# A two-layer decoder trunk on one core: 17 of the 22 gate/up tile pairs of the feed-forward input as seven products of half blocks

## The chip, the core and the metric

The kernel runs on one core of a Trainium2 chip. A core has a matrix engine (PE, with PEld for its weight loads), a vector engine (DVE), a scalar engine (ACT), a general engine (POOL, GpSimd) and a sync engine (SP); each takes its instructions in a fixed order and they wait for one another by semaphores. 16 DMA engines move data between HBM and the on-chip memories SBUF and PSUM. The metric is the device time of one execution in microseconds (us).

## The reference

Two layers, each a norm, a combined input projection, three token mixers (windowed attention, short convolution, a grouped state-space model), a gated merge, an output projection, and then the feed-forward part that the change is about. With 512 tokens, width 1024 and 2816 hidden features, that part is:

```python
h = rmsnorm(x, norm_ffn[i])
gt, up = jnp.split(h @ w_ffn_in[i], 2, axis=-1)
x = x + (jax.nn.silu(gt) * up) @ w_ffn_out[i]
```

All is float32.

## The kernel before

Features lie on the 128 partitions and tokens on the free axis, so x is 8 tiles of 128x512. Each large product is made of three matmuls in the matrix engine's rounded float32 format: every operand is split into a high part (rounded) and a low part (what the rounding left), and high·high, high·low and low·high are summed in PSUM (mm3, L151; gemm runs it over 8 blocks of the inner dimension).

Weights come in chunks of 128x1024 (8 blocks of 128x128; some of 512 columns). SP loads a chunk into a `raw` tile (2 buffers), ACT writes its high part `whi` (L132), DVE its low part `wlo` (L134, 3 buffers each); `chunk()` keeps AHEAD = 2 chunks prepared beyond the one in use.

The feed-forward part of a layer goes through 22 tiles f of 128 hidden features in four groups (FGROUPS: 8, 8, 2 and 4 tiles). For a tile, 24 matmuls of 512 columns give the gate's product `pfg` and 24 more the up product `pfu`, in PSUM banks of a pool of four ("mm"). DVE multiplies both by the token scale of the norm (`ga`, `ub`, L239), ACT takes a tanh (`th`, L959), DVE finishes the silu, multiplies, and ACT and DVE split the hidden tile into high and low parts (L171, L172). After each group its hidden tiles are multiplied by the rows of the output weights (`pfo`, 8 tiles of 128 features) and DVE adds the result to `xres`. The last products of layer 2 go by halves of the tokens, with matmuls of 256 columns.

The order of each engine's instructions is set when the program is built, by a scheduler that plays the program through; buffers of one tag are handed out in that order, and an instruction that takes a buffer over waits for the last reader of what was in it.

Of the kernel before, what the change touches and what calls it, by code (L numbers as in the profile page):

```python
# [16 lines left out]
P = 128  # L17
# [18 lines left out]
# how many units of other work lie between the steps of an octet, of a block of queries, and between these  # L36
# [18 lines left out]
def hybrid_kernel(ctx, tc, xin, wst, vec, ssp, ssb, sbt, cst, out):  # L55
# [6 lines left out]
    ap = ctx.enter_context(tc.tile_pool(name="ap", bufs=1))  # L62
# [4 lines left out]
    NU2 = 61  # L67
    NWP, NRAW, AHEAD = 3, 2, 2
# [22 lines left out]
    # the tables of the activation functions are there before the data  # L91
    A.activation(small([P, 1], "warm"), ones[:, 0:1], AF.Square)

    # the tensor engine's clock is up before the data
# [30 lines left out]
    def chunk_steps():  # L125
        if not raws:
            fetch_chunk()
        raw, cuts = raws.pop(0)
        hi = wp.tile([P, 1024], F32R, tag="whi", bufs=NWP, name="whi")
        lo = wp.tile([P, 1024], F32R, tag="wlo", bufs=NWP, name="wlo")  # L130
        for c in cuts:
            A.copy(hi[:, c], raw[:, c])  # L132
            yield
            V.tensor_tensor(out=lo[:, c], in0=raw[:, c], in1=hi[:, c].bitcast(F32), op=ALU.subtract)  # L134
# [12 lines left out]
    def mm3(o, w, x, start, stop):
        """o += w.T x for w, x given as (high, low) parts."""
        (wh, wl), (xh, xl) = w, x
        for i, (a, b) in enumerate(((wh, xh), (wh, xl), (wl, xh))):  # L150
            T.matmul(o, a, b, start=start and i == 0, stop=stop and i == 2)  # L151
# [34 lines left out]
    def norm_steps(ssum, got, n=NB, bank=auxps):  # L186
        """r[token, block] and r broadcast over partitions (in PSUM), from the partial sums of squares."""
# [74 lines left out]
    first = chunk_steps()  # L262
# [12 lines left out]
    # what is not needed yet does not go before the weights  # L275
# [3 lines left out]
    def u_products(ssum):  # L279
        """The input of the SSM, with the norm of the tokens worked out between its products."""  # L280
# [107 lines left out]
    def sincos_of(y):  # L388
# [168 lines left out]
    def ssm_octet(l, o, ut, store, yso):  # L557
        """Eight groups of the SSM, its steps apart for other work to run between them."""
# [20 lines left out]
        # C lambda^0..3 (imaginary part negated), lambda^1..4 B_bar turned  # L579
# [10 lines left out]
        # responses inside a chunk, D with them  # L590
# [26 lines left out]
        tcs = [tab[:, i, qt] for i in range(2)]  # L617
        # turned back by phi c, the recurrence is real: z_c = |lambda|^4 z_(c-1) + w_c
# [25 lines left out]
        # channels back on the partitions; tokens stay in the order (step, chunk)  # L644
# [61 lines left out]
    def attention(l, n, qkf, vs, kt, ot):  # L706
# [87 lines left out]
    for l in range(DEPTH):  # L794
# [24 lines left out]
        kt = [ap.tile([P, NKV, 2 * P], F32R, tag=f"kt{i}", bufs=1, name=f"kt{i}") for i in range(2)]  # L819
# [125 lines left out]
        xg, ssum = [], None  # L945
        for gi, (f0, f1) in enumerate(FGROUPS):
# [208 lines left out]
```

## Time and profile before

| | |
|---|---|
| time, median of 3 runs | 1594.62 us (1593.84 to 1596.13) |
| the profiled execution: span | 1592.0 us |
| PE busy | 1575.5 us, 99%, 7620 instructions |
| DVE busy | 994.8 us, 62% |
| ACT busy | 565.9 us, 36% |
| POOL busy | 119.0 us, 7% |
| DMA | 165.87 MB, mean 104 GB/s |
| DMA queues | hardware 157.35 MB (30.3% of the 16 engines' time), software, issued by POOL, 6.71 MB (2.0%) |

The span runs from the first to the last instruction on the chip; the rest of the time (2.6 us against the median) lies around it. "Busy" is the time in which at least one instruction of the engine ran; records of PE overlap, since matmuls are pipelined. In the parts below a row of the chain of waits gives start, duration, engine, tile, line and count; a row of the groups gives line, engine, operation, output <- inputs, shape, count, then total busy time and the mean in ns of one; "DMA issues" ends in the median us from issue to landing.

### The profile page before, as it was taken

How to read it: one execution, taken by the hardware profiler on the slowest of the kernel's cores; microseconds unless marked ns; L12 is line 12 of the kernel's file. 1: busy time of each engine (PE TensorE's matmuls, PEld its weight loads, DVE VectorE, ACT ScalarE, POOL GpSimd, SP SyncE). 2: the span in 40 equal slices, each digit the busy share in tenths (PEclk: the TensorE clock that was granted, in tenths of full speed). 3: DMA queues.
4: the chain of work that ended last, by engine and by line, in shares of the span. 5: the costliest groups of instructions: out<-in, count | busy, mean ns of one | idle time of the engine just before them, and what ended most of it. 6: DMA issues, size and time to landing. Idle time of an engine off the chain costs nothing.

```text
span 1592.0 us, 20211 instructions
## 1 busy us (share of the span) xinstructions
PE 1575.5 (99%) x7620; PEld 1301.7 (82%) x7620; DVE 994.8 (62%) x1986; ACT 565.9 (36%) x939; POOL 119.0 (7%) x231
## 2 busy tenths in 40 slices
PE   9999999999999999999999999999999999999996
PEld 7877788888888888888888778788888888888886
DVE  7976779746655345445658676887475643544546
ACT  4355433344432222222424554333443322222223
POOL 0301112210000000000030012212000000000001
PEclk9999999999999999999999999999999999999998
DMA  5422324323423322322433233333243323232231
GB/s 196 135 95 76 96 83 119 119 70 119 152 93 99 100 93 96 104 93 94 157 107 111 76 89 96 93 103 113 70 152 119 95 91 106 93 105 93 94 105 67
DMA packets 69985, 165.87 MB, mean 104 GB/s; under 512 B 18848, under 2 KB 24256, under 8 KB 69888
## 3 DMA queue, kind: packets, MB, share of 16 engines
q1 hardware_dynamic: 62944, 157.35, 30.3%
q0 software_dynamic: 6656, 6.71, 2.0%
q8 instruction: 60, 0.98, 0.2%
q10 hardware_dynamic: 288, 0.52, 0.1%
q14 instruction: 37, 0.30, 0.1%
HBM read 155.10 MB, written 5.24 MB: 101 GB/s over the span
## 4 chain that ended last, share of the span: by engine, by line
PE 98%; DVE 1%; DMA 0%; issue 0%; ACT 0%; SPq 0%; DVEq 0%
PE pg L151 17%; PE pfo L151 15%; PE pfu L151 15%; PE pfg L151 15%; PE pc L151 8%; PE py L151 8%; PE px L151 5%; PE pu L151 3%; PE pqb L151 3%; PE pkv L151 1%; PE pz L151 1%; PE pS L730 1%; PE po L776 1%; PE py L640 1%; PE pvv L614 1%; PE pT L764 1%
## 5 line engine op out<-in xcount | busy, mean ns | idle before, releaser
L132 ACT CAST whi<-raw 128x1024 fp32r<-128x1024 f32 (+1 forms) x298 | 287.8, 967 | 807.2 <-issue 194.2
L134 DVE TENSOR_TENSOR wlo<-raw,whi 128x1024 fp32r<-128x1024 f32 (+1 forms) x298 | 332.9, 1118 | 104.1 <-ACT whi L132 98.0
L151 PE MATMUL pg<-hi,whi 128*128 128x512 f32 x384 | 152.4, 397 | 0.0
L151 PE MATMUL pg<-lo,whi 128*128 128x512 f32 x384 | 150.3, 391 | 0.0
L151 PE MATMUL pg<-hi,wlo 128*128 128x512 f32 x384 | 150.1, 391 | 0.0
L151 PE MATMUL pfo<-lo,whi 128*128 128x512 f32 (+1 forms) x384 | 142.4, 371 | 0.0
L151 PE MATMUL pfo<-hi,wlo 128*128 128x512 f32 (+1 forms) x384 | 142.3, 371 | 0.0
L151 PE MATMUL pfo<-hi,whi 128*128 128x512 f32 (+1 forms) x384 | 140.9, 372 | 0.0
L151 PE MATMUL pfu<-hi,wlo 128*128 128x512 f32 x352 | 137.2, 390 | 0.0
L151 PE MATMUL pfu<-hi,whi 128*128 128x512 f32 x352 | 137.1, 390 | 0.0
L151 PE MATMUL pfu<-lo,whi 128*128 128x512 f32 x352 | 137.0, 389 | 0.0
L151 PE MATMUL pfg<-hi,whi 128*128 128x512 f32 x352 | 136.9, 389 | 0.0
L151 PE MATMUL pfg<-lo,whi 128*128 128x512 f32 x352 | 136.9, 389 | 0.0
L151 PE MATMUL pfg<-hi,wlo 128*128 128x512 f32 x352 | 136.9, 389 | 0.0
L239 DVE TENSOR_TENSOR xres<-xres,pfo 128x512 f32<-128x512 f32 (+1 forms) x72 | 44.0, 626 | 116.2 <-PE pfo L151 115.8
L239 DVE TENSOR_TENSOR ub<-pfu,rb 128x512 f32<-128x512 f32 x44 | 30.4, 691 | 108.6 <-PE pfu L151 108.6
L239 DVE TENSOR_TENSOR ga<-pfg,rb 128x512 f32<-128x512 f32 x44 | 30.4, 691 | 93.2 <-PE pfg L151 93.2
L151 PEld LDWEIGHTS pg<-hi,whi 128*128 128x128 f32 x384 | 72.1, 188 | 16.0 <-issue 1.0
L151 PEld LDWEIGHTS pg<-hi,wlo 128*128 128x128 f32 x384 | 72.1, 188 | 15.2
L151 PEld LDWEIGHTS pg<-lo,whi 128*128 128x128 f32 x384 | 72.2, 188 | 14.2
L151 PEld LDWEIGHTS pfo<-lo,whi 128*128 128x128 f32 x384 | 72.3, 188 | 12.5
L151 PEld LDWEIGHTS pfo<-hi,wlo 128*128 128x128 f32 x384 | 72.3, 188 | 12.5
(244 smaller groups left out, 3043.1 us busy)
## 6 DMA issues: line engine op xcount, KB each, us to landing
raw<-wst SPq DMA_DIRECT2D x240, 512.0 KB, 3.5
raw<-wst SPq DMA_DIRECT2D x56, 256.0 KB, 2.5
x<-xin SPq DMA_DIRECT2D x8, 256.0 KB, 5.1
bt<-sbt SPq DMA_DIRECT2D x8, 256.0 KB, 4.7
pt<-pfd SPq DMA_DIRECT2D x64, 32.0 KB, 4.1
mt<-kd POOLq DMA_DIRECT2D x64, 32.0 KB, 3.8
yd<-yj POOLq DMA_DIRECT2D x64, 32.0 KB, 2.8
xres<-xin SPq DMA_DIRECT2D x8, 256.0 KB, 3.8
```

Source lines behind the costliest of these rows:

```text
L132: A.copy(hi[:, c], raw[:, c])
L134: V.tensor_tensor(out=lo[:, c], in0=raw[:, c], in1=hi[:, c].bitcast(F32), op=ALU.subtract)
L151: T.matmul(o, a, b, start=start and i == 0, stop=stop and i == 2)
L239: V.tensor_tensor(out=out, in0=a, in1=b, op=op)
L614: T.matmul(pv[i][:, q], vt[i][:, q].rearrange("p g s -> p (g s)"), ut[:, q], start=True, stop=True)
L640: T.matmul(py[:, q, 1:NCK], flat(cl[i], q), xs[i][:, q, 0 : NCK - 1], start=False, stop=(i == 1),)
L730: T.matmul(pS[par][:, hp, keys], qt[a][rows, 2 * k + hp], kt[b][rows, k, keys], start=i == 0, stop=i == 2,)
L764: T.transpose(pT[:, h], st[h // 2][:, h % 2, kb * P : (kb + 1) * P], ident)
L776: T.matmul(po[64 * par : 64 * par + 64], v, pt[:, 2 * par : 2 * par + 2], start=kb == 0, stop=kb == len(pts) - 1,)
```

## The change

The groups become 6, 6, 6 and 4 tiles. The first five tiles of a layer (f < NPLAIN = 5) stay as they were, except that the activation is ACT's Silu in place of tanh and two steps of DVE. The other 17 go as a "pair" (`pair_tile`): gate and up weights are the two rows of a block matrix, the inner dimension is halved (4 blocks each), the tokens are halved (256 columns each), and the 2x2 block product is made of seven half-block products in place of eight, in Winograd's form of Strassen's scheme. So a pair is 7 x 4 x 3 = 84 matmuls of 256 columns, where a plain tile is 2 x 8 x 3 = 48 of 512.

For that each layer forms once, from the normed input (`halves_steps`), the halves of the tokens b11, b21, b22 and their sums t1 to t4, each split in high and low parts (DVE and ACT). Of the weights, the sums s1 to s4 are needed beside a11, a12 and a22: SP loads `r2` (a21, a11) from a new array wsp and POOL adds (a22, a21) to it by a DMA that accumulates (L149); DVE makes `r3` from it with two additions (L184, L185); SP loads `r1` (a11, a12) and `r4` (a22) as they are. ACT writes the high parts h1 to h4 (3 of 1024 columns, 1 of 512), DVE the low parts l1 to l4 (L162). While a pair's products run, the steps of a later pair's weights and the evaluation of the pair before are taken in turn (`beside`).

The seven products go to three PSUM tiles: `pb` (a11 b11, then s2 t2 and s3 t3 added on), `pc` (a22 t4) and `pd` (a12 b21 in one half, s1 t1 and s4 b22 in the other). ACT copies pb, the second half of pd, pb again and pc (128x256 each, L1092 to L1099) between the products; then DVE adds, ACT takes Silu (L1106), and DVE finishes (L240 is the last low part).

Buffers: raw 2 to 5, whi and wlo 3 to 5; the general pool `u2` 61 to 62, with a few tiles of other pools moved into it or into raw, whi and wlo. Three more loads of ACT's function tables appear in the program (4 in place of 1). The rest of the diff below the fence is naming, layout on the host and comments.

```diff
-FGROUPS = [(0, 8), (8, 16), (16, 18), (18, 22)]
+FGROUPS = [(0, 6), (6, 12), (12, 18), (18, 22)]
+NPLAIN = 5
+NF = FFN // P
+HS = S // 2
...
-    NU2 = 61
-    NWP, NRAW, AHEAD = 3, 2, 2
+    NU2 = 62
+    NHI, NLO, NRAW, AHEAD = 5, 5, 5, 2
...
     def fetch_chunk(queue=nc.sync, parts=1):
-        i = loaded[0]
+        i, n = items[loaded[0]]
         loaded[0] += 1
-        raw = wp.tile([P, 1024], F32, tag="raw", bufs=NRAW, name="raw")
-        n = sizes[i] // parts
+        if n is None:
+            r1, r2, r4 = wraw("r1"), wraw("r2"), u2([P, S], F32, "r4")
+            queue.dma_start(r2, wsp[i, :, 1024:2048])
+            queue.dma_start(r1, wsp[i, :, 0:1024])
+            nc.gpsimd.dma_start(r2, wsp[i, :, 2048:3072], accum_op=ALU.add)
+            queue.dma_start(r4, wsp[i, :, 2048 : 2048 + S])
+            raws.append((r1, r2, r4))
+            return None
...
+    def lo_of(lo, raw, hi):
+        V.tensor_tensor(out=lo, in0=raw, in1=hi.bitcast(F32), op=ALU.subtract)
+        return lo
+    def item_steps():
         if not raws:
             fetch_chunk()
-        raw, cuts = raws.pop(0)
-        hi = wp.tile([P, 1024], F32R, tag="whi", bufs=NWP, name="whi")
-        lo = wp.tile([P, 1024], F32R, tag="wlo", bufs=NWP, name="wlo")
-        for c in cuts:
-            A.copy(hi[:, c], raw[:, c])
-            yield
-            V.tensor_tensor(out=lo[:, c], in0=raw[:, c], in1=hi[:, c].bitcast(F32), op=ALU.subtract)
-            yield
-        ready.append((hi, lo))
+        got = raws.pop(0)
+        if len(got) == 2:
+            raw, cuts = got
+            hi, lo = whi(), wlo()
+            for c in cuts:
+                A.copy(hi[:, c], raw[:, c])
+                yield
+                lo_of(lo[:, c], raw[:, c], hi[:, c])
+                yield
+            ready.append((hi, lo))
+            return
+        r1, r2, r4 = got
+        a, b = slice(0, S), slice(S, 2 * S)
+        h1 = whi("h1")
+        A.copy(h1, r1)
+        r3 = wraw("r3")
+        V.tensor_tensor(out=r3[:, a], in0=r2[:, a], in1=r1[:, a], op=ALU.add)
+        V.tensor_tensor(out=r3[:, b], in0=r3[:, a], in1=r1[:, b], op=ALU.add)
+        yield
+        h2 = whi("h2")
+        A.copy(h2, r2)
+        p1 = (h1, lo_of(wlo("l1"), r1, h1))
+        yield
+        h3 = whi("h3")
+        A.copy(h3, r3)
+        p2 = (h2, lo_of(wlo("l2"), r2, h2))
+        yield
+        h4 = u2([P, S], F32R, "h4")
+        A.copy(h4, r4)
+        p3 = (h3, lo_of(wlo("l3"), r3, h3))
+        yield
+        p4 = (h4, lo_of(u2([P, S], F32R, "l4"), r4, h4))
+        part = lambda p, c: (p[0][:, c], p[1][:, c])
+        ready.append(
+            dict(a11=part(p1, a), a12=part(p1, b), s1=part(p2, a), s3=part(p2, b),
+                 s2=part(p3, a), s4=part(p3, b), a22=part(p4, a))
+        )
...
+        def halves_steps():
+            for j in range(KT // 2):
+                h1, h2 = u2([P, S], F32, "h1"), u2([P, S], F32, "h2")
+                for h, k in ((h1, j), (h2, j + KT // 2)):
+                    stt(h, xres[k], vcol(l, V_NF, k), rb2, ALU.mult, ALU.mult)
+                yield
+                b11, b12, b21, b22 = h1[:, :HS], h1[:, HS:], h2[:, :HS], h2[:, HS:]
+                t12, t34 = u2([P, 2, HS], F32, "t12"), u2([P, 2, HS], F32, "t34")
+                tt(t12[:, 0], b11, b12, ALU.subtract)
+                stt(t12[:, 1], t12[:, 0], -1.0, b22, ALU.mult, ALU.subtract)
+                tt(t34[:, 0], b22, b12, ALU.subtract)
+                stt(t34[:, 1], t12[:, 1], -1.0, b21, ALU.mult, ALU.subtract)
+                yield
+                first = u2([P, 2, HS], F32R, "b11")
+                A.copy(first[:, 0], b11)
+                tt(first[:, 1], b11, first[:, 0].bitcast(F32), ALU.subtract)
+                parts = []
+                for t in (h2.rearrange("p (a c) -> p a c", a=2), t12, t34):
+                    hi, lo = split(t, None, shape=(P, 2, HS))
+                    parts += [(hi[:, i], lo[:, i]) for i in range(2)]
+                    yield
+                b21_, b22_, t1, t2, t3, t4 = parts
+                ops.append(dict(b11=(first[:, 0], first[:, 1]), b21=b21_, b22=b22_, t1=t1, t2=t2, t3=t3, t4=t4))
+                yield
+        def hidden(ga, ub, hid):
+            tt(ga, ga, ub, ALU.mult)
+            hid.append(split(ga, None))
+        def plain_tile(f, hid):
+            pg, pu = mmps([P, S], "pfg"), mmps([P, S], "pfu")
+            for p_ in (pg, pu):
+                w = chunk()
+                gemm(p_, w, KC, xg2)
+                if f == 0:
+                    next(norm2)
+                yield
+            if f == 0:
+                nonlocal_rb.append(broadcast_of(rs_[1])[0])
+            r = nonlocal_rb[0]
+            ga, ub = u2([P, S], F32, "ga"), u2([P, S], F32, "ub")
+            tt(ga, pg, r, ALU.mult)
+            A.activation(ga, ga, AF.Silu)
+            tt(ub, pu, r, ALU.mult)
+            hidden(ga, ub, hid)
+            yield
+        def pair_tile(hid, beside):
+            if not ready:
+                load_chunk()
+            w = ready.pop(0)
+            pb, pc, pd = mmps([P, HS], "pb"), mmps([P, HS], "pc"), auxps([P, 2, HS], "pd")
+            ga, ub = u2([P, 2, HS], F32, "ga"), u2([P, 2, HS], F32, "ub")
+            def product(o, a, b, start=True):
+                n = len(ops)
+                for k in range(n):
+                    c = KC(k)
+                    mm3(o, (w[a][0][:, c], w[a][1][:, c]), ops[k][b], start and k == 0, k == n - 1, more=not start)
+                for g in list(beside):
+                    if next(g, "end") == "end":
+                        beside.remove(g)
+            product(pb, "a11", "b11")
+            A.copy(ga[:, 0], pb)
+            product(pd[:, 0], "a12", "b21")
+            product(pd[:, 1], "s1", "t1")
+            A.copy(ub[:, 1], pd[:, 1])
+            product(pb, "s2", "t2", start=False)
+            A.copy(ga[:, 1], pb)
+            product(pc, "a22", "t4")
+            A.copy(ub[:, 0], pc)
+            product(pd[:, 1], "s4", "b22", start=False)
+            product(pb, "s3", "t3", start=False)
+            def evacuated():
+                flat = lambda x: x.rearrange("p a c -> p (a c)")
+                tt(ga, ga, pd, ALU.add)
+                A.activation(ga, ga, AF.Silu)
+                yield
+                stt(ub, pb.unsqueeze(1).to_broadcast([P, 2, HS]), -1.0, ub, ALU.mult, ALU.subtract)
+                yield
+                hidden(flat(ga), flat(ub), hid)
+                yield
+            return evacuated()
+        nonlocal_rb = []
+        beside = []
         for gi, (f0, f1) in enumerate(FGROUPS):
             hid = []
             for f in range(f0, f1):
-                pg, pu = mmps([P, S], "pfg"), mmps([P, S], "pfu")
-                for p_ in (pg, pu):
-                    w = chunk()
-                    gemm(p_, w, KC, xg2)
-                    if f == 0:
-                        next(norm2)
-                if f == 0:
-                    rb2, _ = broadcast_of(rs_[1])
-                ga, ub, th = u2([P, S], F32, "ga"), u2([P, S], F32, "ub"), u2([P, S], F32, "th")
-                tt(ga, pg, rb2, ALU.mult)
-                A.activation(th, ga, AF.Tanh, scale=0.5)
-                tt(ub, pu, rb2, ALU.mult)
-                stt(ga, th, 1.0, ga, ALU.add, ALU.mult)
-                tt(ga, ga, ub, ALU.mult)
-                hid.append(split(ga, 0.5))
+                if f < NPLAIN:
+                    for _ in plain_tile(f, hid):
+                        if f == 0 and nonlocal_rb:
+                            rb2 = nonlocal_rb[0]
+                            prep = halves_steps()
+                        elif f > 0:
+                            for _ in range(3):
+                                next(prep, None)
+                    continue
+                if f == NPLAIN:
+                    for _ in prep:
+                        pass
+                if not ready:
+                    load_chunk()
+                if next_is_pair() and f + 1 < f1:
+                    beside.append(item_steps())
+                ev = pair_tile(hid, beside)
```

Where the instructions stand. **DVE, the plain tiles of layer 1.** Of before, from the first evaluation of a tile (`ga<-pfg` is tile 0's, `pfg_4473` and `pfg_4547` are those of tiles 1 and 2; `wlo` low parts of weights):

```order
L134 TENSOR_TENSOR wlo_4508<-raw_4505,whi_4507 128x1024
L239 TENSOR_TENSOR ga_4461<-pfg_4364,rb_4459 128x512
L239 TENSOR_TENSOR ub_4462<-pfu_4365,rb_4459 128x512
L243 SCALAR_TENSOR_TENSOR ga_4461<-th_4463,ga_4461 128x512
L239 TENSOR_TENSOR ga_4461<-ga_4461,ub_4462 128x512
L172 SCALAR_TENSOR_TENSOR lo_4470<-ga_4461,hi_4469 128x512
L239 TENSOR_TENSOR ga_4535<-pfg_4473,rb_4459 128x512
L134 TENSOR_TENSOR wlo_4552<-raw_4549,whi_4551 128x1024
L239 TENSOR_TENSOR ub_4536<-pfu_4474,rb_4459 128x512
```

Of after, the same place; `h1`, `h2`, `t12`, `t34` and `b11` are the halves and their sums, `r3` a weight sum of the first pair:

```order
L162 TENSOR_TENSOR wlo_4624<-raw_4621,whi_4623 128x1024
L313 TENSOR_TENSOR ga_4457<-pfg_4360,rb_4455 128x512
L313 TENSOR_TENSOR ub_4458<-pfu_4361,rb_4455 128x512
L184 TENSOR_TENSOR r3_4852<-r2_4844,r1_4843 128x512
L313 TENSOR_TENSOR ga_4457<-ga_4457,ub_4458 128x512
L185 TENSOR_TENSOR r3_4852<-r3_4852,r1_4843 128x512
L240 TENSOR_TENSOR lo_4464<-ga_4457,hi_4463 128x512
L317 SCALAR_TENSOR_TENSOR h1_4499<-xres_4063,vecs_72,rb_4455 128x512
L317 SCALAR_TENSOR_TENSOR h2_4500<-xres_4226,vecs_72,rb_4455 128x512
L162 TENSOR_TENSOR wlo_4691<-raw_4688,whi_4690 128x1024
L313 TENSOR_TENSOR t12_4503<-h1_4499 128x256
L313 TENSOR_TENSOR t34_4504<-h2_4500,h1_4499 128x256
```

Before, tile 0 is evaluated in five rows and then tile 1; after, the steps of the halves and the first pair's weights stand between. Further on, from the first pair's low part l1 to tile 2's `ga<-pfg` (`pfg_4581`), which frees a PSUM bank, it is 22 rows, and these are the last of them:

```order
L317 SCALAR_TENSOR_TENSOR h1_4651<-xres_4144,vecs_72,rb_4455 128x512
L317 SCALAR_TENSOR_TENSOR h2_4652<-xres_4308,vecs_72,rb_4455 128x512
L313 TENSOR_TENSOR t12_4655<-h1_4651 128x256
L313 TENSOR_TENSOR t34_4656<-h2_4652,h1_4651 128x256
L317 SCALAR_TENSOR_TENSOR t12_4655<-t12_4655,h2_4652 128x256
L313 TENSOR_TENSOR b11_4661<-h1_4651,b11_4661 128x256
L240 TENSOR_TENSOR lo_4665<-h2_4652,hi_4664 128x512
L317 SCALAR_TENSOR_TENSOR t34_4656<-t12_4655,h2_4652 128x256
L313 TENSOR_TENSOR ga_4668<-pfg_4581,rb_4455 128x512
```

**PE, around the first pair of layer 1.** Of before, from the end of tile 4's up product (`pfu_4696`) to the next tile:

```order
L151 MATMUL pfu_4696<-hi_4356,whi_4655 128x512
L151 MATMUL pfu_4696<-lo_4357,whi_4655 128x512
L151 MATMUL pfu_4696<-hi_4356,wlo_4656 128x512
L151 MATMUL pfg_4769<-hi_4070,whi_4699 128x512
L151 MATMUL pfg_4769<-lo_4071,whi_4699 128x512
L151 MATMUL pfg_4769<-hi_4070,wlo_4700 128x512
```

Of after, the end of the pair's `pd` (s1 t1) and what follows; `b11` holds both parts, so that "x2" is two matmuls, and `h4`, `l4` are the parts of a22:

```order
L225 MATMUL pd_4871<-hi_4765,l2_4861 128x256
L225 MATMUL pb_4869<-b11_4509,h1_4850 128x256 x2
L225 MATMUL pb_4869<-b11_4509,l1_4857 128x256
L225 MATMUL pb_4869<-b11_4574,h1_4850 128x256 x2
L225 MATMUL pb_4869<-b11_4574,l1_4857 128x256
L225 MATMUL pb_4869<-b11_4661,h1_4850 128x256 x2
L225 MATMUL pb_4869<-b11_4661,l1_4857 128x256
L225 MATMUL pb_4869<-b11_4728,h1_4850 128x256 x2
L225 MATMUL pb_4869<-b11_4728,l1_4857 128x256
L225 MATMUL pc_4870<-hi_4550,h4_4863 128x256
L225 MATMUL pc_4870<-lo_4551,h4_4863 128x256
L225 MATMUL pfo_4988<-hi_4463,whi_4972 128x512
```

Before, one plain tile follows the other; after, the products of the first pair follow tile 4, and the fourth product (`pc`) and the first output product `pfo_4988` are taken in turn (of its six hidden tiles those of the five plain ones come first, hi_4839 and lo_4840 of tile 4 as the fifth; the pair's own comes later).

**SP, the loads for that place.** Of before:

```order
L121 DMA raw_4653<-wst 128x1024
L121 DMA raw_4697<-wst 128x1024
L121 DMA raw_4727<-wst 128x1024
L121 DMA raw_4771<-wst 128x1024
L121 DMA raw_4801<-wst 128x1024
L121 DMA raw_4845<-wst 128x1024
```

Of after; `raw` of 768 columns are chunks of the output weights, `r1`, `r2` and `r4` belong to pairs (`r4_4845` to the first one, `r2_5179` to the second):

```order
L147 DMA r2_4844<-wsp 128x1024
L148 DMA r1_4843<-wsp 128x1024
L157 DMA raw_4970<-wst 128x768
L157 DMA raw_4976<-wst 128x768
L157 DMA raw_4982<-wst 128x768
L157 DMA raw_5008<-wst 128x768
L157 DMA raw_5034<-wst 128x768
L157 DMA raw_5060<-wst 128x768
L157 DMA raw_5086<-wst 128x768
L157 DMA raw_5112<-wst 128x768
L150 DMA r4_4845<-wsp 128x512
L147 DMA r2_5179<-wsp 128x1024
```

The first pair's `r2` and `r1` stand ahead of the eight chunks of the first group's output weights, its `r4` behind all eight.

More of the change, by code (lines that the diff above doesn't have):

```diff
@@ L54, in hybrid_kernel @@
 @with_exitstack
-def hybrid_kernel(ctx, tc, xin, wst, vec, ssp, ssb, sbt, cst, out):
+def hybrid_kernel(ctx, tc, xin, wst, wsp, vec, ssp, ssb, sbt, cst, out):
     nc = tc.nc
@@ L112, in hybrid_kernel, with wraw, whi, wlo @@
     raws = []
+    def wraw(name="raw", dt=F32):
+        return wp.tile([P, 1024], dt, tag="raw", bufs=NRAW, name=name)
+    def whi(name="whi", dt=F32R):
+        return wp.tile([P, 1024], dt, tag="whi", bufs=NHI, name=name)
+    def wlo(name="wlo", dt=F32R):
+        return wp.tile([P, 1024], dt, tag="wlo", bufs=NLO, name=name)
     def fetch_chunk(queue=nc.sync, parts=1):
-        i = loaded[0]
+        i, n = items[loaded[0]]
         loaded[0] += 1
-        raw = wp.tile([P, 1024], F32, tag="raw", bufs=NRAW, name="raw")
-        n = sizes[i] // parts
+        if n is None:
[6 more added lines that the diff above has]
+            return None
+        raw = wraw()
+        n //= parts
         cuts = [slice(j * n, (j + 1) * n) for j in range(parts)]
@@ L138, in load_chunk, with next_is_pair, mm3 @@
     def load_chunk():
-        for _ in chunk_steps():
+        for _ in item_steps():
             pass
+    def next_is_pair(n=0):
+        i = loaded[0] - len(raws) + n
+        return i < len(items) and items[i][1] is None
     def chunk():
-        while len(ready) <= AHEAD and (raws or loaded[0] < len(sizes)):
+        while len(ready) <= AHEAD and (raws or loaded[0] < len(items)) and not next_is_pair():
+            load_chunk()
+        if not ready:
             load_chunk()
         return ready.pop(0)
-    def mm3(o, w, x, start, stop):
+    def mm3(o, w, x, start, stop, more=False):
@@ L149, in mm3 @@
         (wh, wl), (xh, xl) = w, x
         for i, (a, b) in enumerate(((wh, xh), (wh, xl), (wl, xh))):
-            T.matmul(o, a, b, start=start and i == 0, stop=stop and i == 2)
+            T.matmul(o, a, b, start=start and i == 0, stop=stop and i == 2, skip_group_check=more)
     def gemm(o, w, kcols, xs):
@@ L261, in hybrid_kernel @@
     xg = []
-    first = chunk_steps()
+    first = item_steps()
     with tc.manual_schedule(engines={mybir.EngineType.DVE, mybir.EngineType.Activation}):
@@ L299, in u_evacuated @@
         for o in range(4):
+            if o % 2 == 0:
+                both = whi("uts", F32).rearrange("p (o q c) -> p o q c", o=2, q=4)
             u = u2([P, TJ, NCK], F32, "uperm")
@@ L522, in ssm_params @@
         qs = slice(l * NQ, (l + 1) * NQ)
-        b_c = cp.tile([P, 4, NQ, GRP], F32, tag="b_c", name="b_c")
+        b_c = wraw("b_c").rearrange("p (i q h) -> p i q h", i=4, q=NQ)
         with tc.issue_after(third.ins):
@@ L533, in ssm_tables @@
         qs = slice(l * NQ + half * nq, l * NQ + (half + 1) * nq)
-        tab = cp.tile([P, 2, nq, NCK], F32, tag="tab", name="tab")
-        store.append(tab)
-        tc_, tn_ = tab[:, 0], tab[:, 1]
+        tc_, tn_ = (wlo("tab", F32).rearrange("p (q c) -> p q c", q=nq) for _ in range(2))
+        store.append((tc_, tn_))
         V.memset(tc_[:, :, 0:1], 1.0)
@@ L616, in ssm_octet @@
         qt = slice((o % 2) * 4, (o % 2) * 4 + 4)
-        tcs = [tab[:, i, qt] for i in range(2)]
+        tcs = [tab[i][:, qt] for i in range(2)]
         s4 = lambda name: u2([P, 4, NCK], F32, name)
@@ L818, in hybrid_kernel @@
         vs = u2([P, NB, P], F32, "vs")
-        kt = [ap.tile([P, NKV, 2 * P], F32R, tag=f"kt{i}", bufs=1, name=f"kt{i}") for i in range(2)]
+        kt = [t[:, i] for t in [wraw("kt", F32R).rearrange("p (i v n) -> p i v n", i=2, v=NKV)] for i in range(2)]
         ot = [(u2([P, S], F32R, "oth"), u2([P, S], F32R, "otl")) for _ in range(4)]
@@ L1041, in _pkc, with _tiles, _pairs @@
     return w[:, c0:c1].reshape(k, P, c1 - c0).transpose(1, 0, 2).reshape(P, -1)
+def _tiles(i, l, f):
+    w = i["w_ffn_in"][l]
+    return [_pkc(w, c + f * P, c + (f + 1) * P) for c in (0, FFN)]
+def _pairs(i):
+    st = np.zeros((DEPTH * (NF - NPLAIN), P, 3072), np.float32)
+    for n in range(st.shape[0]):
+        g, u = _tiles(i, n // (NF - NPLAIN), NPLAIN + n % (NF - NPLAIN))
+        (a11, a12), (a21, a22) = ((w[:, :S], w[:, S:]) for w in (g, u))
+        st[n] = np.concatenate([a11, a12, a21, a11, a22, a21], 1)
+    return st
 def _weights(i):
@@ L1146 @@
         nc.dram_tensor(n, arrays[n].shape, F32, kind="ExternalInput").ap()
-        for n in ("xin", "wst", "vec", "ssp", "ssb", "sbt", "cst")
+        for n in ("xin", "wst", "wsp", "vec", "ssp", "ssb", "sbt", "cst")
     ]
```

54 lines of the change are left out of this document (38 added, 16 removed).

## Prediction

> **What bounds the kernel now.** I first read the shares of the chain of waits, then the chain in order of time where the feed-forward part begins, and at the places with matmuls of 256 columns:
>
> ```profile
> PE 98%; DVE 1%; DMA 0%; issue 0%; ACT 0%; SPq 0%; DVEq 0%
> ...
> 52.56 10.92 PE pkv L151 x91
> ...
> 442.13 5.44 PE pfg L151 x24
> 447.57 0.44 PE pr L215 x4
> 448.00 5.47 PE pfu L151 x24
> 453.47 5.44 PE pfg L151 x24
> 458.91 5.44 PE pfu L151 x24
> 464.35 5.44 PE pfg L151 x24
> 469.79 5.44 PE pfu L151 x24
> 475.23 5.44 PE pfg L151 x24
> ...
> 1552.57 15.53 PE pfo L151 x129
> ```
>
> The matrix engine is the chain, and in the feed-forward part one tile follows the other without a gap. 24 matmuls of 512 columns take 5.44 us: 226.7 ns each. Those of 256 columns take 10.92/91 = 15.53/129 = 120 ns. The other engines, by windows over the first two groups (columns: PE, PEld, DVE, ACT, POOL busy us, granted clock, DMA share, GB/s):
>
> ```profile
> 430.00:562.00 132.00, 132.00 (x590) 109.44 (x589) 63.68 (x87) 36.41 (x43) 0.00 (x0) 1.00 0.30 96
> 562.00:693.00 131.00, 131.00 (x580) 108.51 (x579) 60.55 (x73) 34.97 (x41) 0.00 (x0) 1.00 0.29 97
> ```
>
> DVE is busy under half of the stage, ACT a good quarter, DMA 0.30. So fewer PE cycles shorten the stage, as long as DVE, ACT and the loads keep up.
>
> **The matmuls.** A pair: before 48 x 226.7 = 10.88 us, after 84 x 120 = 10.08 us; 0.80 us less. 34 pairs: **-27.2 us**. The 7/8 of the scheme would give 1.36 us a pair, but 512 columns cost 106.7 ns more than 256, so each matmul has 13.3 ns that don't shrink, and there are 36 more. The rule that would make this smaller still, a gap per matmul, stands in the Trainium skill, "TensorE: Matmul & The Clock Gate", section "Wait — 56ns, not 53.3ns?": N/2.4 GHz plus about 2.5 ns. By it a pair would gain 48 x 215.8 - 84 x 109.2 = 1.19 us and the sum here be an estimated -40 us; the rows differ (226.7 and 120 ns), and I go by the rows. The output products keep 528 matmuls a layer whatever the groups: nothing.
>
> **DVE and ACT, steady state.** The durations, from the groups by shape:
>
> ```profile
> L134 DVE TENSOR_TENSOR wlo<-raw,whi 128x1024 fp32r<-128x1024 f32 x240 | 293.1, 1222 | 74.3 <-ACT whi L132 73.4 <-PE pq L709 0.6
> L239 DVE TENSOR_TENSOR ga<-ga,ub 128x512 f32<-128x512 f32 x44 | 30.5, 692 | 1.5
> L172 DVE SCALAR_TENSOR_TENSOR lo<-xres,vecs,hi 128x512 fp32r<-128x512 f32 x24 | 17.8, 747 | 4.8 <-ACT hi L171 4.8
> L239 DVE TENSOR_TENSOR apt<-b_c,pw 128x256 f32<-128x256 f32 x32 | 12.1, 419 | 0.0
> L132 ACT CAST whi<-raw 128x1024 fp32r<-128x1024 f32 x240 | 252.0, 1051 | 689.3 <-issue 185.0 <-PE pfo L151 160.4 <-PE pfg L151 137.5
> L132 ACT CAST whi<-raw 128x512 fp32r<-128x512 f32 x58 | 35.8, 620 | 117.9 <-PE pg L151 72.8 <-PE py L151 26.6 <-issue 9.2
> L171 ACT ACTIVATE hi<-ga 128x512 fp32r<-128x512 f32 x44 | 27.9, 634 | 31.0 <-DVE ga L239 31.0
> L180 ACT ACTIVATE sq<-xres 128x256 f32<-128x256 f32 x16 | 6.3, 414 | 10.5 <-DVE xres L239 10.5
> L92 ACT ACT_TABLE_LOAD x1 | 1.3, 1283 | 1.2 <-PEq L1144 1.2
> ```
>
> A pair costs DVE l1 to l3 3 x 1.22, l4 and two sums 3 x 0.69, evaluation 4 x 0.69: 8.5 us of 10.08. ACT: h1 to h3 3 x 1.05, h4 0.62, four copies 4 x 0.41, Silu and high part 1.27: 6.7 us. Both fit, but tighter than before (5.9 and 3.4 of 10.88), so I cost the pairs at PE's 10.08 us; every us by which DVE passes 10.08 would cost 34. Three more table loads (3 x 1.28 = 3.8 us of ACT) lie where ACT has idle time: nothing, at most 3.8. The buffers that were moved (rb, q, k and tables) touch the mixing part, where PE waits in no row of the chain; 0, with 3 us either way.
>
> **The plain tiles: a first wait.** In the order of after, `ga<-pfg` of tile 2, which frees the bank for tile 4, stands 22 rows behind l1. l1's buffer is free when PE ends tile 2's up product, 464.35 on the clock of before, plus ACT's h1 1.05: 465.40. The 22 rows are two of 1024 columns (2.44), four h1/h2 as L172's with a pointer (2.99), ten of 256 (4.19) and six of 512 (4.15): 13.8 us, to 479.2. How DVE goes through such rows shows the timeline:
>
> ```profile
> 455.56 0.68 DVE L239 TENSOR_TENSOR ub<-pfu,rb 128x512 f32<-128x512 f32 x1
> 456.16 0.68 DVE L243 SCALAR_TENSOR_TENSOR ga<-th,ga 128x512 f32<-128x512 f32 x1
> 456.87 0.69 DVE L239 TENSOR_TENSOR ga<-ga,ub 128x512 f32<-128x512 f32 x1
> ```
>
> Independent rows start 0.60 us apart, 0.08 under their duration; a dependent one 0.71. Over 22 rows that is up to 1.7 us less: 477.5. PE comes to tile 4 at 475.23 plus nine matmuls of the pair, 1.08: 476.3. The wait is 1.2 to 2.9 us; I take **2.4**, nearer the long end, since several of the rows wait on ACT's high parts in between. Not below nothing.
>
> **The first pair: a second wait.** PE then does tile 4 (10.88), pd (15 x 0.12) and pb (12 x 0.12) and comes to pc, whose weights are h4, l4. Their load r4 stands on SP behind the last chunk of the output weights, whose `raw` buffer is freed by the low part of the third chunk (wlo_4985), and that one, with its high part, takes the buffer of PE's a11 product: it begins when PE ends pb. From there, on no other path, with 768 columns halfway between 512 and 1024:
>
> ```profile
> L134 DVE TENSOR_TENSOR wlo<-raw,whi 128x512 fp32r<-128x512 f32 x58 | 39.8, 686 | 29.8 <-ACT whi L132 24.6 <-DMA pt<-pfd 4.8
> ...
> raw<-wst SPq DMA_DIRECT2D x240, 512.0 KB, 3.5
> raw<-wst SPq DMA_DIRECT2D x56, 256.0 KB, 2.5
> ...
> ut<-uperm POOLq DMA_DIRECT2D x48, 32.0 KB, 2.1
> ```
>
> High part 0.84, low part 0.95, r4's 256 KB 2.5, h4 0.62: 4.9 us. Beside it: on DVE behind wlo_4985 stand tile 3's last low part and tile 4's evaluation (4 x 0.69), then ACT's high part 0.63 ahead of h4: 0.84 + 0.95 + 2.76 + 0.63 + 0.62 = 5.8. I take **5.5**; ends 4.9 and 5.8. Layer 2 has the same order: 2 x (2.4 + 5.5) = **+15.8 us**.
>
> **The clock after such a wait.** PE's last records and the windows behind them:
>
> ```profile
> 1576.17 0.35 PE L192 MATMUL pm<-ones,sq 128*128 128x1 f32 x2
> 1577.06 0.83 PE L192 MATMUL pm<-ones,sq 128*128 128x1 f32 x6 [0.53 <-ACT sq L180]
> ...
> 1578.00:1579.00 1.00, 0.00 (x0) 0.00 (x0) 0.96 (x5) 1.00 (x4) 1.00 (x2) 1.00 0.00 0
> 1579.00:1580.00 1.00, 0.00 (x0) 0.00 (x0) 0.93 (x3) 0.66 (x2) 1.00 (x3) 0.65 0.74 262
> 1580.00:1581.00 1.00, 0.00 (x0) 0.00 (x0) 0.97 (x2) 0.00 (x0) 1.00 (x2) 0.50 0.72 262
> ```
>
> 0.65 in the middle window means a fall to half at about 1579.3: 1.4 us after the last small matmuls (1577.9), 3.2 after the steady ones (1576.1). So it falls within a 5.5 us wait. No row shows the return; if it takes as long as the fall, half of 1.4 to 3.2 us is lost, 0.7 to 1.6; I take 1.2 a layer, **+2.4 us**. The same page of the Trainium skill, section "Part 1: The HAM clock gate", says the clock halves after an idle window of about 3.4 us and returns after as long a busy one. The tail's rows agree with the fall; by its figure the loss would be an estimated 1.7 us a layer, 3.4 in all.
>
> **Sum.** -27.2 + 15.8 + 2.4 = -9.0 us, on the profiled span of 1592.0: 1583.0. Times of the runs lie 2.6 us above it (median 1594.62): **1585.6 us**. The ends of the two waits and the clock, 2 x (1.2 + 4.9 + 0.7) = 13.6 and 2 x (2.9 + 5.8 + 1.6) = 20.6, with the tables and 3 us for the mixing, give 1578 to 1595.
>
> **Rivals.** *The waits don't come* (0.17). If r4 arrives in time and DVE gets through the preparation, all of -27.2 is kept: 1567.4. For it: DVE has 54% idle in the stage. Against it: the idle time is before a buffer comes free, and the order is fixed.
>
> *The accumulating DMA is slow* (0.15). No row of before accumulates. Its bounds: the plain 512 KB load, 3.5 us; and by the queues and POOL's issue of one such DMA
>
> ```profile
> q1 hardware_dynamic: 62944, 157.35, 30.3%
> q0 software_dynamic: 6656, 6.71, 2.0%
> ...
> L606 POOL DMA_DIRECT2D mt<-kd x64 | 33.5, 531 | 27.5 <-DMA kd<-kpad 7.7 <-PE pS L730 7.3 <-issue 6.6
> ```
>
> software DMA takes 0.020 x 1592/6.71 = 4.75 us per MB against 3.07, so 0.52 MB 2.5 us behind a start of 2.1 (the `ut` row): 4.6, and 7.1 if each byte is moved twice. I take 4.6. It matters so: l2 of pair n+1 frees the buffer, r2 of pair n+3 loads (3.5), is accumulated, and its sum r3 (0.69) stands on DVE ahead of l2 of pair n+2 (1.22). Such a round must stay under 10.08, so load, issue (0.53) and accumulate under 8.2; as the weights are prepared some 1.3 pairs ahead, a group of six (four rounds) bears 3.1 more, 11.3: an accumulate of 7.3. At 9 us, four groups of six lose 4 x 1.7 x 4 = 27 us: 1585.6 + 27 = 1613, slower.
>
> *ACT's copies come late* (0.11). PE adds s4 b22 onto pd only when ACT has copied it, 60 matmuls (7.2 us) into the pair. ACT's copy stands behind the high part of the pair before, which waits for DVE: 0.69 (ub), 1.9 (a sum and l2), 0.69, then 0.63 and 0.41 on ACT: 4.3 us. It decides from 2.9 us of further lateness on; 0.6 us a pair would then be 20 us: 1606.
>
> **How the numbers follow.** Forecast 0.57, rivals 0.17, 0.15, 0.11. A measurement of this kernel tells 0.2%, 3.2 us, from no change: faster is below 1591.4, slower above 1597.8. Faster: 0.17 and 0.48 of the forecast's cases; same 0.10: its upper end, and a little of the rivals; slower the rest, 0.25. The range goes from the first rival's 1567.4 to the late copies' 1606 and leaves out the slow accumulate.
>
> **What the profile would show.** 34 x 84 matmuls 120 ns apart; in each layer PE gaps near 2 and 5.5 us around tile 4 and the first pc, released by `ga<-pfg` and by h4, and a granted clock under 1 behind the longer one; pairs at 10.1 us, DVE near 80% in them; accumulates landing in 4 to 7 us. I am wrong if the pairs don't run at 10.1, if gaps sit inside them (released by h2 or r3: the accumulate; by L1095: the copies), or if there are no gaps.

## The result, and the profile after

The changed kernel takes 1622.57 us (median of 4 runs, 1620.82 to 1628.15), the kernel before 1595.09 us beside it: 1.0179 times as long, 95% interval 1.0161 to 1.0197. The profiled execution of after has a span of 1619.9 us, 27.9 more than before.

The shares of the chain, and PE's largest waits in the whole kernel (total us, times, longest):

```profile
PE 79%; DMA 11%; DVE 7%; issue 2%; ACT 1%; DVEq 0%; SPq 0%; ACTq 0%; POOLq 0%
...
PE pd L225 <- ACT ub L1095: 13.7, 10, 3.0
PE pc L225 <- ACT h L196: 13.1, 2, 6.6
PE pb L225 <- ACT ga L1097: 5.6, 3, 3.0
...
PE pfg L225 <- DVE ga L313: 0.9, 2, 0.4
PE pd L225 <- DVE lo L240: 0.9, 2, 0.4
```

Before, PE was 98% of the chain; now 21% of it lies elsewhere. New are the wait for h4, 6.6 us in each layer, and 13 waits inside the pairs for ACT's copies, 19.3 us.

Where the time went by stage: the chain at the start of layer 1's feed-forward part (pfg), of layer 2 (pu), of its feed-forward part and PE's last output product. Of before:

```profile
430.29 4.76 PE pfg L151 x21
...
790.79 16.32 PE pu L151 x72
...
1213.84 4.76 PE pfg L151 x21
...
1568.44 7.67 PE pfo L151 x63
```

Of after:

```profile
434.91 4.76 PE pfg L225 x21
...
805.39 16.32 PE pu L225 x72
...
1228.09 4.76 PE pfg L225 x21
...
1599.93 0.86 PE pfo L225 x7
```

| stage | before | after | difference |
|---|---|---|---|
| to the first feed-forward part | 430.3 | 434.9 | +4.6 |
| feed-forward, layer 1 | 360.5 | 370.5 | +10.0 |
| mixing, layer 2 | 423.1 | 422.7 | -0.4 |
| feed-forward, layer 2 | 362.3 | 372.7 | +10.4 |
| behind PE's last output product | 15.9 | 19.1 | +3.2 |

The matmuls are as forecast, 120 ns each (the last row of the fence below: 24 in 2.88 us). A layer's part should have been 13.6 us shorter by them and is 10 longer, so some 24 us a layer were lost: 18.6 and 16.2 us in the two layers to PE's waits, 2.4 and 5.2 to a halved clock behind some of them (worked out in the account of the prediction); the last 2 to 3 us of each are not accounted for. What fills the chain in the pairs is a sequence of transfers, with DVE between them. The chain in the second group of layer 1:

```profile
519.88 6.63 DMA r<-wsp
...
531.51 6.28 DMA r<-wsp
...
541.04 5.52 DMA r<-wsp
...
554.27 5.58 DMA r<-wsp
561.79 3.61 DMA r<-wsp
565.96 5.51 DMA r<-wsp
577.62 5.65 DMA r<-wsp
...
599.47 2.88 PE pd L225 x24
```

and DVE's timeline there (`l` of 560.55 and of 572.16 are the l2 of two pairs that follow one another, `r<-r,r` the first addition to r3):

```profile
559.94 0.69 DVE L184 TENSOR_TENSOR r<-r,r 128x512 f32<-128x512 f32 x1 [4.46 <-DMA r<-wsp]
560.55 1.22 DVE L162 TENSOR_TENSOR l<-r,h 128x1024 fp32r<-128x1024 f32 x1
...
567.24 0.68 DVE L317 SCALAR_TENSOR_TENSOR ub<-pb,ub 128x512 f32<-128x512 f32 x1
571.55 0.69 DVE L184 TENSOR_TENSOR r<-r,r 128x512 f32<-128x512 f32 x1 [3.63 <-DMA r<-wsp]
572.16 1.22 DVE L162 TENSOR_TENSOR l<-r,h 128x1024 fp32r<-128x1024 f32 x1
573.30 0.68 DVE L313 TENSOR_TENSOR ga<-ga,ub 128x512 f32<-128x512 f32 x1
```

l2 ends at 561.7, the load into its buffer runs from 561.79 for 3.61 us, the accumulate from 565.96 for 5.51, r3's addition starts as it lands, and the next l2 stands behind that: a round of 11.6 us (560.55 to 572.16), where PE needs 10.08. Behind l2 on DVE stands the evaluation of the pair before (`ga<-ga,ub`), on whose high part ACT's copies wait, and PE on these. That is my theory A. Rivals: the accumulating DMA costs by itself, by what it takes from the others; or DVE's and ACT's own load makes the copies late.

### The profile page after: what moved, and what is told of

It reads as the page before. It is cut to its first block, busy times and chain, and to the rows that moved or that the text cites. A ratio compares the mean times of both kernels' runs of the same rounds, so it can differ in the third digit from the quotient of the medians.

```text
span 1619.9 us, 23473 instructions
## 1 busy us (share of the span) xinstructions
PE 1562.7 (96%) x8844; PEld 1346.3 (83%) x8844; DVE 1099.7 (68%) x2170; ACT 682.4 (42%) x1190; POOL 148.1 (9%) x265
## 3 DMA queue, kind: packets, MB, share of 16 engines
q0 software_dynamic: 11552, 24.54, 8.6%
## 4 chain that ended last, share of the span: by engine, by line
PE 79%; DMA 11%; DVE 7%; issue 2%; ACT 1%; DVEq 0%; SPq 0%; ACTq 0%; POOLq 0%
PE pg L225 16%; DMA r<-wsp 10%; PE pc L225 10%; PE pfo L225 10%; PE py L225 8%; PE px L225 5%; PE pd L225 5%; PE pb L225 5%; PE pu L225 3%; PE pfg L225 3%; PE pfu L225 3%; PE pqb L225 2%; PE pkv L225 1%; PE pz L225 1%; DVE l L162 1%
## 5 line engine op out<-in xcount | busy, mean ns | idle before, releaser
L173 ACT CAST whi<-raw 128x1024 fp32r<-128x1024 f32 (+2 forms) x242 | 216.4, 903 | 385.1 <-PE pg L225 103.6
L162 DVE TENSOR_TENSOR wlo<-raw,whi 128x1024 fp32r<-128x1024 f32 (+2 forms) x242 | 250.3, 1039 | 84.0 <-ACT whi L173 68.1
L162 DVE TENSOR_TENSOR l<-r,h 128x1024 fp32r<-128x1024 f32 (+1 forms) x136 | 146.8, 1086 | 34.8 <-ACT h L196 25.2
L225 PE MATMUL pd<-hi,h 128*128 128x256 f32 x408 | 117.0, 287 | 13.7 <-ACT ub L1095 13.7
L225 PE MATMUL pd<-lo,h 128*128 128x256 f32 x408 | 116.2, 285 | 0.9 <-DVE lo L240 0.9
L225 PE MATMUL pd<-hi,l 128*128 128x256 f32 x408 | 116.0, 284 | 0.0
L149 POOL DMA_DIRECT2D r<-wsp x34 | 29.1, 856 | 801.9 <-DMA r<-wsp 318.1
L184 DVE TENSOR_TENSOR r<-r,r 128x512 f32<-128x512 f32 x34 | 23.5, 690 | 107.3 <-DMA r<-wsp 107.2
L225 PEld LDWEIGHTS pd<-hi,h 128*128 128x128 f32 x408 | 78.5, 192 | 15.9 <-ACT ub L1095 15.7
L225 PEld LDWEIGHTS pg<-hi,whi 128*128 128x128 f32 x384 | 72.1, 188 | 16.2 <-issue 0.8
L225 PEld LDWEIGHTS pfo<-hi,whi 128*128 128x128 f32 x384 | 73.1, 191 | 13.2 <-ACT hi L239 0.7
L225 PE MATMUL pb<-hi,h 128*128 128x256 f32 x272 | 78.1, 287 | 5.6 <-ACT ga L1097 5.6
```

Of the source, the lines that this page charges most:

```text
L149: nc.gpsimd.dma_start(r2, wsp[i, :, 2048:3072], accum_op=ALU.add)
L162: V.tensor_tensor(out=lo, in0=raw, in1=hi.bitcast(F32), op=ALU.subtract)
L184: V.tensor_tensor(out=r3[:, a], in0=r2[:, a], in1=r1[:, a], op=ALU.add)
```

## The experiments

**The rest of the change alone.** No pairs; NPLAIN = 22 and the halves left out.

```diff
-NPLAIN = 5
+NPLAIN = 22
...
-                        elif f > 0:
-                            for _ in range(3):
-                                next(prep, None)
...
```

> All 22 tiles plain, no halves are formed; groups of 6, 6, 6, 4, Silu and the new buffers stay. In the changed kernel's profile the part ahead of the first feed-forward tile is 4.6 us longer than before (434.9 against 430.3) and the part behind PE's last product 3.2 us longer. Theory A (the buffers and table loads cost this, the pairs have no part in it): 1595.1 + 7.8 = 1603. Theory B (only the front is theirs, the tail is another matter): 1599.7. Theory C (all of the loss is in the pairs): 1595, no difference from before.

Measured: 1597.86 us, 1.0017 times before (1.0008 to 1.0027). Between B and C: 2.7 us belong to the rest of the change (groups, Silu, buffers, table loads; these were not taken apart). The front of its profile is 3.3 us longer than before's (pfg at 433.58), its end is as before; so the 3.2 us at the end of after belong to something that this kernel lacks.

**No accumulate.** The accumulating DMA left out.

```diff
-            nc.gpsimd.dma_start(r2, wsp[i, :, 2048:3072], accum_op=ALU.add)
```

> Leaves out the accumulating DMA, so s1 and s3 lack an addend; all matmuls, splits and loads stay. Theory A (buffer, load, accumulate, r3, l2 make a round of 11.65 us against PE's 10.08, and this holds the pairs): DVE no longer waits at r3, pairs run at 10.1 us, each layer's feed-forward part falls from 372 to about 355 us (the wait for h4 of 6.6 us stays): about 1590. Theory B (only the waits that PE shows inside the pairs, 11.1 and 8.2 us, hang on it, the rest is PE's own pace): 1603. Theory C (ACT's copies are late by ACT's and DVE's own load): no change, 1622.

Measured: 1591.23 us, 0.9979 (0.9970 to 0.9988), 31 us under after, 3.2 of them at the end of the span. As theory A has it. PE's waits in its trace:

```profile
PE pc L224 <- ACT h L195: 12.4, 2, 6.2
PE pr L288 <- DVE n_y L283: 5.0, 1, 5.0
PE pc L224 <- ACT qr L767: 1.7, 1, 1.7
```

The pr is at the end of the kernel, as before, the qr in the mixing. No wait of PE for a copy is left, though ACT and DVE do all their work of after: their own load is not what makes the copies late. The wait for h4 is untouched.

**The sums made by POOL.** Everything that they need is on the chip: s1 = a21 + r4, s3 = a21 + r1's half.

```diff
-            queue.dma_start(r2, wsp[i, :, 1024:2048])
+            queue.dma_start(r2[:, 0:S], wsp[i, :, 1024 : 1024 + S])
...
-            nc.gpsimd.dma_start(r2, wsp[i, :, 2048:3072], accum_op=ALU.add)
...
+            nc.gpsimd.tensor_tensor(out=r2[:, S:], in0=r2[:, 0:S], in1=r1[:, 0:S], op=ALU.add)
+            nc.gpsimd.tensor_tensor(out=r2[:, 0:S], in0=r2[:, 0:S], in1=r4, op=ALU.add)
```

> The same sums, made by POOL with two additions of 128x512 from a21, r1 and r4, which are on the chip anyway; no accumulating DMA, 1.0 MB less to load per pair, and r4 of the first pair is loaded ahead of the output weights. POOL's 128x256 took 0.72 us, so two of 512 about 2.9 us a pair, beside a round of load 4 + 2.9 + 1.9 = 8.8 us, under 10.08. Theory A: pairs at 10.1 us and no wait for h4: 1590 - 13 = about 1577. Theory C (own load of ACT and DVE): about 1609, only the h4 waits gone. If POOL's additions slow DVE down by sharing the memory port, over 1600.

**The sums made by DVE.** The same two additions on the vector engine, ahead of r3's; the loads are those of the POOL version.

```diff
...
+        V.tensor_tensor(out=r2[:, b], in0=r2[:, a], in1=r1[:, a], op=ALU.add)
+        V.tensor_tensor(out=r2[:, a], in0=r2[:, a], in1=r4, op=ALU.add)
```

> The same sums made by DVE (two more additions of 0.69 us a pair, so DVE 9.9 by durations, near 9.2 by spacing, of 10.08), no accumulating DMA, r4 early. Theory A: the round is short, DVE fits just: 1577 to 1590. Theory C (DVE is what limits the pairs): slower than the changed kernel's pairs, about 1620 or more.

Measured: 1579.30 us with POOL, 0.9906 (0.9889 to 0.9922), and 1579.76 us with DVE, 0.9910 (0.9894 to 0.9925). Both beat both kernels, near what theory A gave. In both, SP now also loads the first pair's r4 ahead of the output weights (PE's waits for h4 are 3.0 and 2.6 us in all, against 13.1), so two things changed at once; the runs below take them apart. DVE holds even 9.9 us of work a pair (by durations). POOL's additions are not free for DVE; the groups of the POOL version, and the same of after:

```profile
L151 POOL TENSOR_TENSOR r<-r,r 128x512 f32<-128x512 f32 x34 | 59.7, 1756 | 79.2 <-DMA r<-wsp 76.2 <-DVE r L185 0.6
...
L163 DVE TENSOR_TENSOR l<-r,h 128x1024 fp32r<-128x1024 f32 x102 | 142.4, 1397 | 16.5 <-ACT h L193 11.6 <-ACT h L189 2.9 <-ACT h L183 2.1
```

```profile
L162 DVE TENSOR_TENSOR l<-r,h 128x1024 fp32r<-128x1024 f32 x102 | 123.9, 1220 | 9.2 <-ACT h L182 7.4 <-ACT h L188 1.5
```

A low part of 1024 columns takes 1397 ns there against 1220 in after and 1219 in the DVE version; PE hardly sees it.

**The accumulate kept, DVE's order changed.** The additions to r3 queue behind the last l2.

```diff
...
+        with tc.issue_after(last_l2[0].ins) if last_l2 else nullcontext():
             V.tensor_tensor(out=r3[:, a], in0=r2[:, a], in1=r1[:, a], op=ALU.add)
...
```

> The accumulating DMA stays; only DVE's order changes: the first addition to r3 of pair n+3, which waits for the accumulate, now stands behind l2 of pair n+2 and not ahead of it. Theory A (the loss is the round l2, load 3.6, accumulate 5.5, r3, l2, closed by this place on DVE): from l2 of one pair to l2 of the next, DVE then has load, issue and accumulate, 9.8 us, which just fits 10.08: pairs near 10.1 us, about 1591 to 1597. Rival (the accumulating DMA costs by itself, by what it takes from the other loads and engines, wherever DVE waits for it): 1610 or more.

Measured: 1595.53 us, 1.0006 (0.9996 to 1.0016), 27 us under after, with all 34 accumulates in place (5.9 us from issue to landing, 5.7 in after). DVE's timeline in the same group:

```profile
566.07 1.22 DVE L197 TENSOR_TENSOR l<-r,h 128x1024 fp32r<-128x1024 f32 x1
567.63 0.69 DVE L187 TENSOR_TENSOR r<-r,r 128x512 f32<-128x512 f32 x1 [0.35 <-DVE l L197]
568.24 0.69 DVE L318 TENSOR_TENSOR ga<-ga,ub 128x512 f32<-128x512 f32 x1
...
576.87 1.22 DVE L197 TENSOR_TENSOR l<-r,h 128x1024 fp32r<-128x1024 f32 x1
578.36 0.69 DVE L187 TENSOR_TENSOR r<-r,r 128x512 f32<-128x512 f32 x1 [0.27 <-DVE l L197]
```

l2 comes first, the addition's wait shrinks from 3.63 us to 0.35, and no wait of PE for ACT's copies is left; that for h4 stays (13.2 us in all). So the accumulate's length alone was not the loss: it was the place, ahead of l2, of the addition that waits for it.

**r4 first.** SP loads the first pair's r4 ahead of the output weights.

```diff
...
+            with tc.issue_after(first_r4[0].ins) if first_r4 else nullcontext():
                 dma = queue.dma_start(raw[:, c], wst[i, :, c])
...
```

> Only SP's order changes: the first pair's r4 of each layer is loaded ahead of the output weights. Theory A (the h4 wait is r4's place on SP's queue, 6.6 us in each layer, and has nothing to do with the round of the accumulate): that wait falls to the 1.3 to 1.6 us that the kernels with r4 early showed, 2 x 5 us less and about 1 us of clock each: about 1611. Rival (tile 4's evaluation and its high part on ACT end as late as r4): 1 to 2 us in all, 1621.

Measured: 1613.65 us, 1.0122 (1.0100 to 1.0144), 9 us under after. Nearer theory A, but the waits for h4 stay at 4.7 us in all, and those for the copies rose from 19.3 to 23.3 us: the round took back a part.

**Both orders.** The two edits together.

> Both changes of order at once, nothing else: r4 of the first pair ahead of the output weights on SP, and r3's additions behind l2 on DVE. All accumulating DMAs stay. Theory A (two places of waiting, each with its price: 27 us for the round, about 5 us of wait and 2.2 us of half clock in each layer for h4): 1595.5 - 14 = about 1581, with the end of the span still 3.3 us longer than without accumulating DMAs. Rival (with the round gone the other wait only moves, as it did in part when r4 alone was moved, 9 us of 14): 1587 or more.

Measured: 1584.90 us, 0.9936 (0.9919 to 0.9952): 10.6 us under the order of DVE alone, between the two expectations. The waits for h4 are 4.7 us in all, as with r4 first alone, and no wait for the copies came back; the two places add up (9 and 27 us alone, 38 together, against after). What stays of h4's wait shows ACT's timeline in layer 1: the high part of tile 4 waits for DVE, and h4 (`h<-r`) stands behind it.

```profile
498.07 0.62 ACT L246 CAST hi<-ga 128x512 fp32r<-128x512 f32 x1 [0.82 <-DVE ga L320]
498.59 0.61 ACT L203 CAST h<-r 128x512 fp32r<-128x512 f32 x1
```

**One plain tile fewer.** The POOL version with NPLAIN = 4.

```diff
-NPLAIN = 5
+NPLAIN = 4
```

> The version with POOL's sums, with four plain tiles in place of five, so two pairs more in the kernel. If the halves are still ready in time: 2 x 0.8 us less than 1579.3, about 1577.7. If the plain tiles are what covers the forming of the halves: PE waits for the t sums and loses some of 10.9 us in each layer: 1585 or more.

Measured: 1592.34 us, 0.9987 (0.9978 to 0.9997), 13 us above the POOL version. PE waits at the first pc again:

```profile
PE pc L226 <- ACT h L197: 12.7, 2, 6.3
```

and the chain ahead of it (layer 1) is DVE forming the halves (h, t, lo) and then evaluating tile 3:

```profile
482.60 1.33 DVE h L318 x2
...
486.94 1.53 DVE lo L241
...
489.77 1.72 DVE ga L314
...
492.10 0.62 ACT h L197
```

Five plain tiles cover all but 3.0 us of that work, four do not.

## Why the prediction was wrong, step by step

It forecast 1585.6 us, faster; the kernel is slower, by the mechanism of its second rival at a much smaller price of the accumulate than that rival asked for. In its order:

- **The matmuls** were right: 120 ns in the pairs, and where the round is gone most of the gain shows: with POOL's sums layer 1's part takes 350.2 us (432.95 to 783.16), 10.3 of the 13.6 shorter than before. The Trainium skill's gap of 2.5 ns ("TensorE: Matmul & The Clock Gate", "Wait — 56ns, not 53.3ns?") is again not what the rows show, 13.3 ns.
- **The steady pairs at PE's pace: the step that failed.** The sum took the accumulate at 4.6 us; it lands in 5.7 in the median (bounds given: 3.5 to 7.1; on the chain 5.2 to 7.7). That is the smaller error. The larger is the bound it was held against: load, issue and accumulate under 8.2 us, *plus 3.1 for weights prepared some 1.3 pairs ahead*, so that only an accumulate over 7.3 us would cost. In the round shown 3.6 + 0.6 + 5.5 = 9.7 us lie between l2 and the addition, under that 11.3, and yet the order on DVE cost 24.5 us (span of after, 1619.9, against 1595.4 with the changed order; 27.0 between the medians). The lead was one of weights, and in the pairs PE waits for no weights but h4: apart from 0.4 us a layer for the halves, its other waits there, 13 of them, are for ACT's copies. On ACT the copies stand behind the high part of the pair before, which needs `ga<-ga,ub`, and that stands on DVE behind the addition: it waits for the accumulate too, however early the weights are. PE first waits in the group's second pair:

```profile
563.40 0.39 PE L225 MATMUL pd<-hi,h 128*128 128x256 f32 x1 [1.38 <-ACT ub L1095]
```

  There the addition had waited 4.46 us (559.94 in the timeline above); in the next pair it waits 3.63 us and PE 0.56. Either way some 3.1 us were spare on this path, about the 2.9 that the prediction gave it under its third rival; the accumulate's wait was never set against them. Without the lead the step's own terms, 3.5 + 0.5 + 4.6 + 1.9 = 10.5 us, would have passed PE's 10.08 by themselves. The rounds were uneven: 11.6 us in this group, 13.3 in the next (accumulates from 662.52 and 675.83, 7.1 and 7.7 us long). PE's 13 waits are 0.2 to 3.0 us long and 19.3 in sum; 3.4 more went with the clock, as said below.
- **ACT's copies late** (third rival) is how PE feels it, but the load of ACT and DVE is not the cause: without the accumulate, or with the other order, the copies come in time.
- **The first wait**: forecast 2.4 us a layer (1.2 to 2.9), measured about 1.1: tile 4's first matmul was due at 476.3 + 4.6 = 480.9 and starts at 482.04. That is just under the low end.

```profile
482.04 0.50 PE L225 MATMUL pfg<-hi,whi 128*128 128x512 f32 x1 [0.43 <-DVE ga L313]
```

- **The second wait**: forecast 5.5 (4.9 to 5.8), measured 6.6 and 6.5. The place and its two causes were right: with r4 early, tile 4's evaluation remains. Mis-sized was r4's load, put at 2.5 us by a row of before; it takes 3.7 on the chain (498.66 to 502.40 us).
- **The clock**: forecast 1.2 a layer; behind h4's wait it was about 2.4 us in layer 1 and 1.8 in layer 2 (missing share of the clock times PE's busy share, summed over windows of 1 us). Windows of after, layer 1 (PE idle from 496.5 to 503.07):

```profile
500.00:501.00 1.00, 0.00 (x0) 0.00 (x0) 0.70 (x2) 0.24 (x2) 0.00 (x0) 1.00 0.94 300
501.00:502.00 1.00, 0.00 (x0) 0.00 (x0) 0.51 (x1) 0.45 (x1) 0.00 (x0) 0.55 0.53 202
502.00:503.00 1.00, 0.00 (x0) 0.00 (x0) 0.18 (x1) 0.60 (x2) 0.00 (x0) 0.50 0.00 0
503.00:504.00 1.00, 0.93 (x3) 0.93 (x4) 0.69 (x1) 0.56 (x3) 0.00 (x0) 0.50 0.00 0
...
507.00:508.00 1.00, 1.00 (x4) 0.73 (x3) 0.00 (x0) 0.00 (x0) 0.00 (x0) 0.54 0.00 0
508.00:509.00 1.00, 1.00 (x6) 0.83 (x5) 0.00 (x0) 0.00 (x0) 0.00 (x0) 1.00 0.00 0
```

  PE ran 4.9 us at half clock (503.07 to 507.9), its 512 columns 427 ns apart, before the clock came back; in layer 2 it was 3.6 us. By the same page of the Trainium skill, Part 1, about 3.4 us of busy time bring it back; the four returns of this trace took 3.4 to 4.9. The sum had no term for the other two: inside layer 2's pairs the clock fell to 0.50 behind waits of 1.8 and 3.0 us for the copies (windows 1381 to 1386 and 1470 to 1474), some 1.7 us lost each time.
- **The rest**: 3 us for the mixing either way covers the 2.7 us of the all-plain kernel, but not the 4.6 us by which the front of after is longer; the end of the span was in no term.

## What to carry to other kernels

When a buffer that comes free starts a chain of transfers, and what waits for that chain stands on an in-order engine ahead of the instruction that frees the next buffer, it is a round: compare its whole length with the time of one step of the work, and ask of everything that stands behind the waiting instruction on that engine how late it may come. Weights prepared ahead were no help to an evaluation that had 3 us to spare. Then look at the order before the transfer: here moving two additions behind one row was worth 27 us, nearly as much as taking the accumulates out (31 us). Where the operands of a sum are on the chip anyway, two additions of 0.7 us on an engine with room did better than a transfer of 5.7 us: 1579.76 us, against 1584.90 for the best order that keeps the accumulates; 3.2 us of this difference lie at the end of the span.

## What the runs showed of the hardware

- An accumulating DMA of 512 KB into SBUF landed 5.7 us after its issue, a plain load of the same array 4.1. The software queue's time per MB rose with them: 0.086 x 1619.9/24.54 = 5.7 us, against 4.75 before.

```profile
q0 software_dynamic: 11552, 24.54, 8.6%
...
r<-wsp SPq DMA_DIRECT2D x68, 512.0 KB, 4.1
...
r<-wsp POOLq DMA_DIRECT2D x34, 512.0 KB, 5.7
```

- The kernels that accumulate end later behind their last output. SP's last issues in after, in the version without accumulates beside it:

```profile
1602.88 9.01 SPq L1195 DMA_DIRECT2D out<-yout  x8
```

```profile
1574.92 9.01 SPq L1194 DMA_DIRECT2D out<-yout  x8
```

  From the end of these to the end of the span it is 8.0 us in after (1611.9 to 1619.9) and 4.8 us without accumulates (1583.9 to 1588.7). All four kernels with accumulates show the longer end (8.0 to 8.1), the other six, before among them, the shorter (4.7 to 5.1). Why was not tried.
- A pause of 2.2 us was followed by a fall of the clock too: with both orders PE waits 2.2 us for h4 in layer 1 (to 499.26), and the windows of 2 us from 498 to 504 show 0.91, 0.50 and 0.73, a fall some 2.6 us behind PE's last matmul. In layer 1 of after and at the end of before it came 4.6 and 1.4 us behind.
